# Two-layer mixer encoder: banks copied to SBUF, wide sums of squares, rotations on VectorE, new places for the MLA heads

## The chip, the core and the metric

The kernel runs on one core of a Trainium2 chip. The metric is the device time of one execution in microseconds. A core has TensorE (PE, matrix products, results in PSUM banks of 128 partitions x 512 fp32), ScalarE (ACT), VectorE (DVE), GpSimd (POOL) and SyncE (SP, which here only starts DMA transfers). Each engine works through its own queue in order and waits for others by semaphores.

## What is computed

Two layers over 256 tokens of width 2048, all in fp32. With `rms` a normalisation by the root of the mean square and a gain, each layer is

```python
h = rms_norm(x, norm_mix)
z = einsum('bsd,de->bse', h, w_in)          # split into ten parts
y_a = mlstm_mixer(...)                       # 4 heads, two directions, gates, dv = 128
y_b = mla_mixer(...)                         # 6 heads: q (128 + 64 rotated) from a 384 latent, k and v from a 128 latent
y_c = dilated_mixer(...)                     # 6 heads, softmax over three dilated bands
x = x + einsum('bse,ed->bsd', concatenate([y_a, y_b, y_c]), w_out)
h = rms_norm(x, norm_ff)
u = relu(einsum('bsd,df->bsf', h, w_ff1))
return x + einsum('bsf,fd->bsd', u * u, w_ff2)
```

In `mla_mixer` both latents are normalised, each head's q and k parts are normalised over their own columns, the 64-wide parts are rotated (`x1*cos - x2*sin`, `x2*cos + x1*sin`), and a full softmax attention follows.

## The kernel before

**Products.** Every fp32 operand is split into a high part that TensorE takes at full rate (fp32r) and the rest: high x high, high x low, low x high, three products in place of one. Weights come as tiles of 128 x 1024 fp32 (512 KB) by SP's DMA queue. `Weights.next` keeps three tiles staged (`wst`) and splits three units ahead: ScalarE casts `whi`, VectorE subtracts `wlo`. One such unit feeds 12 products of 512 columns (`token_group`). Tokens are two tiles of 128 (`tt`).

**Stages of a layer.** `mixers` runs nine groups of eight units over `w_in`: group 0 the latents (512 columns), group 1 narrow (336 columns: the 64 rotated k columns, gates, part of the dilated v), groups 2 to 4 the mLSTM q/k, v and output gate, 5 to 7 dilated q/k by pairs of heads, 8 the rest of dilated v. Then `out_proj`, then `ffn` in four chunks. In the first layer x comes transposed (`xt`), and `first_xg` makes the operands and the sums of squares of the first norm on POOL (`sq`, `acc`); `token_factor` turns them into the factor `rt` that evictions apply.

**The order of the work** is fixed while the program is written out. Small work is a set of generator tasks in `Stream`. `issue` keeps a clock for each engine from the prices in `Engine.COST`, `product` one for TensorE; a task's next step is due when its last operation is priced to have ended, plus `MARGIN`, and `pump` inserts the steps that are due between products. `finish`, `until` and `start` do not wait for a due time: they write out the steps of other tasks at once until a condition holds. Rooms are counted (`take`, `give`): `m` for the four PSUM banks of small work, `t2` and `half` for SBUF tiles.

**MLA heads.** `mla_head` starts at places `MLA_AT`, (group, unit), as hooks in `token_group`, through `start`, so it needs its room at that place: two banks, three `t2`, three of seven `half`. It keeps its two banks until the normalised q and k (`nk`) are written. Six squares with accumulated sums on ScalarE give the norms, POOL rotates (`apply_rope`), then transposes (`nkT`, `qrT`), scores (`mla_s`), softmax, transposes of it (`pT`) and the product with v (`oT`). In the profile's line column all ScalarE, VectorE and POOL operations have line 98 (the call in `Engine`), products line 194 (`mm`) and transposes line 200; so the tiles' names tell operations apart.

```python
MLA_AT = ((2, 3), (2, 7), (3, 3), (3, 7), (4, 3), (4, 7))
MLA_ROOM = dict(m=2, t2=3, half=3)
self.until(lambda: all(self.room[k] >= v for k, v in room.items()))   # in Stream.start
```

Of the kernel before, what the change touches and what calls it, by code (L numbers as in the profile page):

```python
# [66 lines left out]
T2, HALF = 22, 7  # L67

MLA_AT = ((2, 3), (2, 7), (3, 3), (3, 7), (4, 3), (4, 7))
MARGIN = 0.4  # L70


class Engine:
# [3 lines left out]
        "activation": (0.16, 0.00083), "copy": (0.07, 0.00083), "tensor_tensor": (0.07, 0.00104),  # L77
        "scalar_tensor_tensor": (0.13, 0.00104), "tensor_scalar": (0.07, 0.00080), "tensor_copy": (0.07, 0.00104),
        "tensor_reduce": (0.07, 0.00104), "tensor_tensor_reduce": (0.07, 0.00104), "reciprocal": (0.07, 0.0066),
        "tensor_tensor_scan": (0.07, 0.00104), "memset": (0.07, 0.0004),  # L80
    }

# [3 lines left out]
    def __getattr__(self, f):  # L86
# [4 lines left out]
        def call(*args, **kw):  # L91
            out = kw["in_"] if f == "tensor_reduce" else kw["out"] if "out" in kw else args[0]
            n = math.prod(out.shape[1:])
            fixed, each = self.COST[f]
            if self.name == "pool":
                fixed, each = 0.15, 2 * each
            self.s.issue(self.name, fixed + each * n)
            return fn(*args, **kw)  # L98
# [18 lines left out]
class Stream:  # L117
# [98 lines left out]
class Weights:  # L216
# [7 lines left out]
    def load(self):  # L224
# [111 lines left out]
def first_xg(c, xg, kt, src, gain):  # L336
# [11 lines left out]
    c.s.cur.last.pop("pool", None)  # L348
# [5 lines left out]

def next_xg(c, xg, g, ss, col):

    nc = c.nc
    for tt in range(NT):
        j = c.tmp.tile([P, 512], F32, tag="junk5", name="junk5", bufs=1)
        nc.scalar.activation(j, c.x[tt][:, g * 512:(g + 1) * 512], AF.Square, accum_out=ss[:, tt, g:g + 1])  # L360
# [72 lines left out]
def token_factor(c, rt):  # L433
# [54 lines left out]
def latents(c, ps, rt, tf):  # L488

    nc = c.nc  # L490
    yield from c.s.take(t2=4)
    while not tf.over:
        yield
# [3 lines left out]
    for tt in range(NT):  # L497
        nc.scalar.activation(z[:, tt, :MLA_QR], ps[tt][:, :MLA_QR], AF.Square, scale=rt[:, tt:tt + 1],
                             accum_out=ss[:, tt:tt + 1])
        nc.scalar.activation(z[:, tt, MLA_QR:], ps[tt][:, MLA_QR:512], AF.Square, scale=rt[:, tt:tt + 1],  # L500
# [9 lines left out]
    for tt in range(NT):  # L510
        nc.scalar.activation(z[:, tt, :MLA_QR], ps[tt][:, :MLA_QR], AF.Copy, scale=f[:, 0, tt:tt + 1])
        nc.scalar.activation(z[:, tt, MLA_QR:], ps[tt][:, MLA_QR:512], AF.Copy, scale=f[:, 1, tt:tt + 1])
# [823 lines left out]
```

## Time and profile before

| | us |
|---|---|
| median of three runs | 2157.35 (2154.82 to 2157.42) |
| the profiled execution | 2155.49 |
| its span, first to last instruction | 2153.3 |
| PE busy | 2119.8 (98%) |
| DVE, ACT, POOL busy | 1322.4, 1082.3, 110.4 |
| mean granted TensorE clock | 0.997 |

The profiled execution lies 1.9 us below the median and 2.2 us above its own span. Busy is the union of an engine's records; a product's record lasts longer than the distance to the next product's start, because products overlap. The stages by the stretches of the trace: the first layer's groups 0 and 1 end near 48 us, its other mixer groups near 291, its output projection near 380, its FFN near 1070; the second layer repeats this, 1360 and 1448 being the ends of its mixers and projection.

### The profile page before, as it was taken

To read this page: it belongs to the slowest core of one execution; us is meant where nothing else is said; L and a number is where in the kernel's file an instruction comes from. 1 tells how busy PE (TensorE), PEld (TensorE's weight loads), DVE (VectorE), ACT (ScalarE), POOL (GpSimd) and SP (SyncE) were. 2 spreads that over 40 slices of the span, in tenths; PEclk is the share of its full clock that TensorE was granted. 3 is DMA by queue.
4 is the path that set the end of the run, shared out by engine and by line. 5 is a ranking of instruction groups with operands and counts; after the bars stand their busy time and mean duration, and the time that the engine had idled before them with its cause. 6 is when DMAs were issued, how large, how long until landed. Compare 5 with 4: busy or idle time off the path is not lost.

```text
span 2153.3 us, 28894 instructions
## 1 busy us (share of the span) xinstructions
PE 2119.8 (98%) x10848; PEld 1804.9 (84%) x10848; DVE 1322.4 (61%) x1963; ACT 1082.3 (50%) x1883; POOL 110.4 (5%) x142
## 2 busy tenths in 40 slices
PE   8999999999999999999999999999999999999999
PEld 6788888888888888888887888888888888888887
DVE  7668755655564565565557687556546655655654
ACT  5666655543453444454456676554434434534442
POOL 6112100000000000000001121000000000000000
PEclk9999999999999999999999999999999999999999
DMA  7544455566656666566554444556565666566565
GB/s 228 189 141 126 154 175 181 187 194 190 193 186 195 194 188 193 190 192 196 178 174 142 143 128 153 174 189 192 186 198 189 190 191 195 187 195 194 187 200 162
DMA packets 109004, 389.89 MB, mean 181 GB/s; under 512 B 12352, under 2 KB 12480, under 8 KB 108608
## 3 DMA queue, kind: packets, MB, share of 16 engines
q1 hardware_dynamic: 107136, 384.97, 56.6%
q10 hardware_dynamic: 1728, 3.07, 0.4%
q8 instruction: 85, 1.39, 0.3%
q14 instruction: 55, 0.45, 0.1%
HBM read 385.90 MB, written 2.10 MB: 180 GB/s over the span
## 4 chain that ended last, share of the span: by engine, by line
PE 89%; ACT 4%; DVE 3%; POOL 2%; issue 1%; DMA 1%; POOLq 0%; ACTq 0%; DVEq 0%; SPq 0%
PE g L194 84%; ACT junk L98 1%; PE mla_z L194 1%; ACT whi L98 1%; DVE wlo L98 1%; POOL acc L98 1%; PE oT L194 1%; POOL sq L98 1%; DMA wst<-w_in 1%; PE xT L200 0%; PE pT L200 0%; PE dil_s L194 0%; PE mla_s L194 0%; POOL rp L98 0%; ACT dil_z L98 0%
## 5 line engine op out<-in xcount | busy, mean ns | idle before, releaser
L98 DVE TENSOR_TENSOR wlo<-wst,whi 128x1024 fp32r<-128x1024 f32 (+2 forms) x732 | 889.5, 1224 | 317.4 <-ACT whi L98 307.7
L98 ACT CAST whi<-wst 128x1024 fp32r<-128x1024 f32 (+2 forms) x732 | 761.2, 1043 | 539.7 <-PE g L194 402.5
L194 PE MATMUL g<-whi,u 128*128 128x512 f32 x2048 | 633.4, 389 | 0.0
L194 PE MATMUL g<-xg,whi 128*128 128x512 f32 x2048 | 489.8, 391 | 0.0
L194 PEld LDWEIGHTS g<-whi,u 128*128 128x128 f32 x2048 | 384.5, 188 | 79.6
L194 PEld LDWEIGHTS g<-xg,whi 128*128 128x128 f32 x2048 | 376.4, 188 | 72.8
L194 PE MATMUL g<-wlo,u 128*128 128x512 f32 x1024 | 398.4, 389 | 0.0
L194 PE MATMUL g<-whi,xg 128*128 128x512 f32 (+1 forms) x1152 | 371.7, 389 | 6.3 <-ACT whi L98 6.3
L194 PEld LDWEIGHTS g<-xg,wlo 128*128 128x128 f32 x2048 | 263.1, 191 | 12.1 <-ACT xg L98 2.0
L194 PE MATMUL g<-xg,wlo 128*128 128x256 f32 x2048 | 267.4, 283 | 1.1 <-ACT xg L98 1.1
L194 PEld LDWEIGHTS g<-whi,xg 128*128 128x128 f32 x1152 | 215.5, 189 | 44.0 <-ACT whi L98 6.3
L194 PEld LDWEIGHTS g<-wlo,u 128*128 128x128 f32 x1024 | 192.3, 188 | 39.8
L194 PE MATMUL g<-wlo,xg 128*128 128x512 f32 (+1 forms) x576 | 222.0, 385 | 3.3 <-DVE wlo L98 3.3
L98 ACT COPY ev<-g 128x256 f32<-128x256 f32 x128 | 48.0, 375 | 340.7 <-PE g L194 340.7
L98 DVE TENSOR_TENSOR ev<-g,ev 128x256 f32<-128x256 f32 x128 | 54.4, 425 | 229.8 <-ACT ev L98 229.7
L194 PE MATMUL g<-whi,y 128*128 128x512 f32 x512 | 162.8, 393 | 0.0
L194 PEld LDWEIGHTS g<-wlo,xg 128*128 128x128 f32 x576 | 109.1, 189 | 23.3 <-DVE wlo L98 6.7
L194 PEld LDWEIGHTS g<-whi,y 128*128 128x128 f32 x512 | 96.1, 188 | 19.7
L194 PE MATMUL g<-wlo,y 128*128 128x512 f32 x256 | 99.7, 389 | 0.0
L98 DVE SCALAR_TENSOR_TENSOR x<-g,r,x 128x512 f32<-128x512 f32 x64 | 45.8, 751 | 83.2 <-PE g L194 83.2
L98 DVE SCALAR_TENSOR_TENSOR ev<-ev 128x256 f32<-128x256 f32 x128 | 54.4, 425 | 4.4
L194 PEld LDWEIGHTS g<-wlo,y 128*128 128x128 f32 x256 | 48.1, 188 | 9.5
(206 smaller groups left out, 1199.1 us busy)
## 6 DMA issues: line engine op xcount, KB each, us to landing
wst<-w_ff SPq DMA_DIRECT2D x512, 512.0 KB, 4.2
wst<-w_in SPq DMA_DIRECT2D x128, 512.0 KB, 3.7
wst<-w_out SPq DMA_DIRECT2D x64, 512.0 KB, 4.2
wst<-w_in SPq DMA_DIRECT2D x16, 336.0 KB, 3.0
wst<-w_mla SPq DMA_DIRECT2D x12, 416.0 KB, 3.1
xt<-xT SPq DMA_DIRECT2D x8, 256.0 KB, 5.1
x<-x SPq DMA_DIRECT2D x2, 1024.0 KB, 7.1
out<-x ACTq DMA_DIRECT2D x8, 256.0 KB, 2.2
```

What stands on the lines that cost most here:

```text
L98: return fn(*args, **kw)
L194: c.nc.tensor.matmul(out, lhsT, rhs, start=start, stop=stop)
```

## The change

- The prices in `COST` are raised, an engine's operations may overlap by 0.08 us, ScalarE's accumulated sums get a price, `MARGIN` is 0.3 in place of 0.4, and a product is priced at n/2400 + 0.0133 us.
- `latents` and `mla_head` copy their PSUM banks to SBUF at once and give them back; MLA gets two SBUF tiles `z` (room `z`), `half` has 9 tiles in place of 7, `t2` 21 in place of 22; an MLA head takes two `t2`. At most two mLSTM heads run at a time (`ml`).
- Sums of squares of MLA and dilated heads: one wide square on ScalarE, then `tensor_reduce` on VectorE.
- `apply_rope` and the gains of the output gate move from POOL to VectorE. The cast of v's high part moves from VectorE to ScalarE.
- `MLA_AT` becomes (3,2), (3,3), (3,7), (4,3), (5,0), (6,1).
- The squares of the first norm move from POOL, beside group 0, to ScalarE and VectorE, after group 0. What needs `rt` in group 1 becomes a task, `narrow`; `finish(tf)` goes.
- The first x load goes to ScalarE's DMA queue, the first weight tile is loaded and split in two halves, ten products of 128 columns stand at the program's start, and the tokens' two loads of 1 MB move from before group 2 to before groups 4 and 5.
- In the very last unit all products of the first token tile stand ahead of those of the second.

```diff
-T2, HALF = 22, 7
-MLA_AT = ((2, 3), (2, 7), (3, 3), (3, 7), (4, 3), (4, 7))
-MARGIN = 0.4
+T2, HALF, MLA_Z, JUNK = 21, 9, 2, 2
+MLA_AT = ((3, 2), (3, 3), (3, 7), (4, 3), (5, 0), (6, 1))
+MARGIN = 0.3
+ML_AT_ONCE = 2
+WARM = 10
...
-        "activation": (0.16, 0.00083), "copy": (0.07, 0.00083), "tensor_tensor": (0.07, 0.00104),
+        "activation": (0.26, 0.00086), "copy": (0.19, 0.00084), "tensor_tensor": (0.155, 0.00105),
...
-    c.s.product(n / 2400.0 * (1 if lhsT.dtype == F32R else 4) + 0.0025)
+    c.s.product(n / 2400.0 + 0.0133 if lhsT.dtype == F32R else n / 1200.0 + 0.0025)
...
+    def pieces(self, i):
+        n = self.srcs[i][1]
+        return [slice(0, n // 2), slice(n // 2, n)] if i == 0 else [slice(0, n)]
...
 def first_xg(c, xg, kt, src, gain):
...
-        sq = c.tmp.tile([P, S], F32, tag="sq", name="sq", bufs=1)
-        nc.gpsimd.tensor_tensor(out=sq, in0=src, in1=src, op=ALU.mult)
-        nc.gpsimd.tensor_tensor(out=c.acc, in0=c.acc, in1=sq, op=ALU.add)
...
+def square(c, src):
+    sq = junk5(c)[:, :src.shape[-1]]
+    c.nc.scalar.activation(sq, src, AF.Square)
+    return sq
...
+def token_factor(c, rt, first):
...
+        xs = [t.rearrange("p i s -> p (i s)") for t in c.xts]
+        for i in range(0, len(xs) + 2, 2):
+            for a in xs[i:i + 2]:
+                nc.scalar.activation(a, a, AF.Square)
+            for a in xs[max(i - 2, 1):i]:
+                nc.vector.tensor_tensor(out=xs[0], in0=xs[0], in1=a, op=ALU.add)
+            yield
...
+def warm_up(c):
+    ones = c.big.tile([P, P], F32, tag="big", name="ones")
+    c.nc.vector.memset(ones, 1.0)
+    ps = new_bank(c, "warm")
+    for _ in range(WARM):
+        c.nc.tensor.matmul(ps[:, :P], ones, ones, start=True, stop=True)
...
 def latents(c, ps, rt, tf):
...
+    for tt in range(NT):
+        nc.scalar.copy(z[:, tt], ps[tt])
     yield from c.s.take(t2=4)
     while not tf.over:
         yield
...
 def apply_rope(c, out, x, cos, sin, n, rot):
...
-    nc.gpsimd.tensor_tensor(out=v1, in0=x, in1=cos, op=ALU.mult)
+    nc.vector.tensor_tensor(out=v1, in0=x, in1=cos, op=ALU.mult)
...
+def narrow(c, ps, rt, tf):
+    while not tf.over:
+        yield
...
+    c.s.spawn(dil_v(c, [p[:, 80:G1_W] for p in ps], rt, slice(0, 256)))
+    c.s.spawn(k_rope(c, z1))
+    c.s.spawn(ml_gates(c, z1))
...
-MLA_ROOM = dict(m=2, t2=3, half=3)
+MLA_ROOM = dict(m=2, t2=2, half=3, z=1)
...
+    for tt in range(NT):
+        nc.scalar.copy(z[:, tt], ps[tt][:, :WZ])
+    c.s.give(m=2)
...
-            nc.scalar.activation(junk(c, b - a), ps[tt][:, a:b], AF.Square, accum_out=ss[:, i, tt:tt + 1])
+    sq = [square(c, z[:, tt, :WQ + MLA_NOPE]) for tt in range(NT)]
...
+            nc.vector.tensor_reduce(out=ss[:, i, tt:tt + 1], in_=sq[tt][:, a:b], op=ALU.add, axis=AX.X)
...
+    nc.scalar.copy(vh, zv)
     apply_rope(c, qr, qr, c.rope[:, 0], c.rope[:, 1], NT, MLA_ROPE)
+    nc.vector.tensor_tensor(out=vl, in0=zv, in1=vh.bitcast(F32), op=ALU.subtract)
...
     for tt in range(NT):
         transpose(c, tq[:MLA_ROPE, tt * P:(tt + 1) * P], qr[:, tt])
     yield
+    c.s.give(z=1)
...
 def dil_prep(c, ps, rt, pair):
...
-        for i in range(4):
-            nc.scalar.activation(junk(c, DIL_DH), z[:, tt, i], AF.Square, accum_out=ss[:, tt, i:i + 1])
+        sq = square(c, z[:, tt].rearrange("p a b -> p (a b)"))
+        yield
+        nc.vector.tensor_reduce(out=ss[:, tt], in_=sq.rearrange("p (a b) -> p a b", a=4), op=ALU.add, axis=AX.X)
...
+            nc.vector.tensor_tensor(out=o, in0=o, in1=c.vec[:, V_ON + h * ML_DV:V_ON + (h + 1) * ML_DV], op=ALU.mult)
...
 def ml_head(c, h):
...
+    yield from c.s.take(t2=2, half=1, ml=1)
     kk, qq, ql = c.mlqk[h]
-    yield from c.s.take(t2=2, half=1)
...
     ps = in_group(c, G1_W)
-    s.finish(tf)
...
-    if after:
-        after()
+    c.kr = None
+    s.spawn(narrow(c, ps, rt, tf))
...
     s.spawn(ml_v(c, ps, rt))
+    if after:
+        after(0)
     ps = in_group(c, 512, hooks(4))
+    if after:
+        after(1)
...
+            if last_layer and ch == NCHUNK - 1 and g == NX - 1:
+                token_group(c, us, ps, 512, range(KT // 2 - 1))
+                last_unit(c, us, ps, 512)
...
+    load_x(nc.scalar)
+    c.w.load()
+    for i in range(c.B_ST - 1):
         load_x()
         c.w.load()
```

## Rows read from the trace of the kernel before

**Rows 1.** Page, part 1: busy us and share of the span of each engine.

```profile
PE 2119.8 (98%) x10848; PEld 1804.9 (84%) x10848; DVE 1322.4 (61%) x1963; ACT 1082.3 (50%) x1883; POOL 110.4 (5%) x142
```

**Rows 2.** Stretches: us, busy of PE, PEld, DVE, ACT, POOL, clock, DMA share, GB/s.

```profile
6.34:12.39 6.05, 5.35 (x12) 3.88 (x13) 6.05 (x6) 4.87 (x9) 5.66 (x6) 1.00 1.01 368
12.39:36.40 24.01, 21.57 (x94) 16.41 (x92) 20.44 (x19) 10.39 (x16) 22.29 (x25) 1.00 0.74 244
36.40:48.00 11.60, 11.60 (x79) 11.58 (x79) 7.58 (x18) 7.58 (x21) 5.52 (x14) 1.00 0.58 166
48.00:98.00 50.00, 47.58 (x259) 39.86 (x258) 33.84 (x80) 34.64 (x91) 3.89 (x7) 1.00 0.60 200
98.00:110.00 12.00, 8.90 (x45) 7.27 (x45) 8.03 (x18) 7.12 (x23) 1.80 (x3) 0.72 0.30 87
110.00:161.00 51.00, 50.35 (x292) 43.31 (x291) 34.67 (x76) 33.02 (x93) 6.88 (x10) 1.00 0.46 148
161.00:291.00 130.00, 125.90 (x669) 106.12 (x668) 101.50 (x229) 85.84 (x237) 21.40 (x20) 1.00 0.45 142
1166.00:1178.00 12.00, 8.71 (x45) 7.33 (x44) 8.07 (x17) 6.77 (x21) 2.16 (x3) 0.72 0.28 91
1178.00:1360.00 182.00, 177.33 (x965) 150.51 (x965) 136.61 (x307) 119.88 (x332) 28.07 (x30) 1.00 0.46 145
```

**Rows 3.** Timeline of the start: start us, us, engine, operation.

```profile
4.09 0.91 ACT L98 ACTIVATE xg<-xt,vec 128x256 fp32r<-128x256 f32 x2 [2.08 <-DMA vec<-vecs]
...
6.34 0.80 PE L194 MATMUL g<-whi,xg 128*128 128x512 f32 x1 [6.34 <-ACT whi L98]
...
7.83 0.79 PE L194 MATMUL g<-wlo,xg 128*128 128x512 f32 x1 [0.70 <-DVE wlo L98]
```

**Rows 4.** Waits of PE: us in total, times, longest us.

```profile
PE pT L200 <- DVE sm_e L98: 5.4, 2, 2.9
PE dqkT L200 <- POOL dil_z L98: 4.4, 4, 1.2
```

**Rows 5.** VectorE's groups, 6.3 to 36.4 us: busy us, mean ns.

```profile
L98 DVE TENSOR_TENSOR wlo<-wst,whi 128x1024 fp32r<-128x1024 f32 x8 | 13.3, 1671 | 0.1
```

**Rows 6.** VectorE's groups, 48 to 380 us.

```profile
L98 DVE TENSOR_TENSOR wlo<-wst,whi 128x1024 fp32r<-128x1024 f32 x92 | 113.3, 1244 | 25.0 <-ACT whi L98 24.6
...
L98 DVE TENSOR_TENSOR y<-oT,y 128x256 fp32r<-128x256 f32 x12 | 5.0, 422 | 6.3 <-ACT y L98 6.3
...
L98 DVE TENSOR_REDUCE sm<-mla_s 128x2 f32<-128x512 f32 x6 | 4.1, 690 | 6.6 <-PE mla_s L194 6.6
...
L98 DVE TENSOR_TENSOR mla_vl<-mla_z,mla_vh 128x128 fp32r<-128x128 f32 x12 | 3.5, 291 | 0.4
```

**Rows 7.** ScalarE's groups, 48 to 380 us.

```profile
L98 ACT CAST whi<-wst 128x1024 fp32r<-128x1024 f32 x93 | 96.7, 1050 | 49.8 <-PE g L194 23.2 <-DMA wst<-w_in 17.7 <-DMA wst<-w_out 5.1
...
L98 ACT CAST p_hi<-pT 128x512 fp32r<-128x512 f32 x12 | 7.0, 591 | 12.8 <-PE pT L200 12.8
...
L98 ACT ACTIVATE junk<-mla_z 128x128 f32<-128x128 f32 x24 | 6.7, 278 | 1.0 <-PE mla_z L194 0.5
...
L98 ACT ACTIVATE junk<-x 128x512 f32<-128x512 f32 x8 | 5.0, 629 | 1.8 <-DVE x L98 1.7
```

**Rows 8.** POOL's groups, whole span.

```profile
L98 POOL TENSOR_TENSOR rp<-dil_z,drope 128x256 f32<-128x256 f32 x12 | 17.9, 1511 | 108.2 <-DVE dil_z L98 102.2 <-DVE ml_den L98 6.0
```

**Rows 9.** Timeline, first layer: a weight cast; the first MLA head.

```profile
63.88 1.05 ACT L98 CAST whi<-wst 128x1024 fp32r<-128x1024 f32 x1 [5.00 <-DMA wst<-w_in]
...
67.26 0.34 PE L194 MATMUL mla_z<-whi,lat_hl 128*128 128x192 f32 x1
...
90.61 0.38 PE L200 MATMUL qrT<-const,qr 128*64 128x128 f32 x2
...
103.67 0.58 PE L194 MATMUL oT<-p_hi,mla_vh 128*128 128x256 f32 x1 [0.25 <-ACT p_hi L98]
```

**Rows 10.** Timeline of the end.

```profile
2148.61 1.43 DVE L98 SCALAR_TENSOR_TENSOR x<-g,r,x 128x512 f32<-128x512 f32 x2 [7.89 <-PE g L194]
```

More of the change, by code (lines that the diff above doesn't have):

```diff
@@ L95, in call @@
             if self.name == "pool":
-                fixed, each = 0.15, 2 * each
-            self.s.issue(self.name, fixed + each * n)
+                fixed, each = 0.3, 4 * each
+            elif self.name == "act" and kw.get("accum_out") is not None:
+                fixed += self.READ
+            self.s.issue(self.name, fixed + each * n, self.OVERLAP)
             return fn(*args, **kw)
@@ L352, in first_xg, with junk5, squares @@
     xg[kt] = hl
+def junk5(c):
+    return c.tmp.tile([P, 512], F32, tag="junk5", name="junk5", bufs=JUNK)
+def square(c, src):
+    sq = junk5(c)[:, :src.shape[-1]]
+    c.nc.scalar.activation(sq, src, AF.Square)
+    return sq
+def squares(c, tt, g, ss):
+    j = junk5(c)
+    c.nc.scalar.activation(j, c.x[tt][:, g * 512:(g + 1) * 512], AF.Square, accum_out=ss[:, tt, g:g + 1])
 def next_xg(c, xg, g, ss, col):
@@ L358, in next_xg @@
     for tt in range(NT):
-        j = c.tmp.tile([P, 512], F32, tag="junk5", name="junk5", bufs=1)
-        nc.scalar.activation(j, c.x[tt][:, g * 512:(g + 1) * 512], AF.Square, accum_out=ss[:, tt, g:g + 1])
+        squares(c, tt, g, ss)
     for half in range(2):
@@ L380, in two_banks, with last_unit @@
     return [c.gps.tile([P, 512], F32, tag="g", name="g") for _ in range(NT)]
+def last_unit(c, acts, ps, w):
+    hi, lo = c.w.next()
+    for tt in range(NT):
+        for j in range(2):
+            kt = KT - 2 + j
+            wh, wl = hi[:, j * w:(j + 1) * w], lo[:, j * w:(j + 1) * w]
+            xh = acts[kt][:, tt * P:(tt + 1) * P]
+            xl = acts[kt][:, S + tt * P:S + (tt + 1) * P]
+            mm(c, ps[tt], xh, wh, False, False)
+            mm(c, ps[tt], xh, wl, False, False)
+            mm(c, ps[tt], xl, wh, False, j == 1)
+            c.s.pump()
 def token_group(c, acts, ps, w, kps=range(KT // 2), hooks=None, prepare=None):
@@ L630, in mla_head @@
         c.s.give(t2=4)
+    z = c.zp.tile([P, 2 * WZ], F32, tag="mla_zs", name="mla_zs").rearrange("p (t w) -> p t w", t=NT)
     ps = []
@@ L637, in mla_head @@
             else:
-                o, cs, first, last = b[:, WQ:WQ + 256], slice(NK * WQ, NK * WQ + 256), True, True
+                o, cs, first, last = b[:, WQ:WZ], slice(NK * WQ, NK * WQ + 256), True, True
             xh = c.lat[kt][:, tt * P:(tt + 1) * P]
@@ L699, in mla_head @@
     p = yield from softmax(c, sc, (MLA_NOPE + MLA_ROPE) ** -0.5, None)
-    yield from pv(c, p, [(vh[:, st], vl[:, st]) for st in range(NT)], 4 + h, 3)
+    yield from pv(c, p, [(vh[:, st], vl[:, st]) for st in range(NT)], 4 + h, 2)
     c.s.give(half=3)
@@ L998, in ml_head @@
     split(c, c.y[h], tp[:, :S])
-    c.s.give(m=1, t2=1, half=1)
+    c.s.give(m=1, t2=1, half=1, ml=1)
 def mixers(c, prepare, after):
@@ L1014, in mixers @@
     ps = in_group(c, 512, prepare=prepare)
-    tf = s.spawn(token_factor(c, rt))
+    tf = s.spawn(token_factor(c, rt, after))
     lat = s.spawn(latents(c, ps, rt, tf))
     ps = in_group(c, G1_W)
-    s.finish(tf)
-    z1 = c.cp.tile([P, NT, MLA_ROPE + 16], F32, tag="z1", name="z1", bufs=1)
-    for tt in range(NT):
-        nc.scalar.activation(z1[:, tt], ps[tt][:, :80], AF.Copy, scale=rt[:, tt:tt + 1])
-    s.spawn(dil_v(c, [p[:, 80:G1_W] for p in ps], rt, slice(0, 256)))
-    kr = s.spawn(k_rope(c, z1))
-    s.spawn(ml_gates(c, z1))
-    if after:
-        after()
+    c.kr = None
+    s.spawn(narrow(c, ps, rt, tf))
     def mla0():
         s.finish(lat)
-        s.finish(kr)
+        s.until(lambda: c.kr)
         mla(0)()
@@ L1110, in ff1_end @@
     yield
-    t = c.tmp.tile([P, S], F32, tag="ev1", name="ev1", bufs=2)
+    t = junk5(c)[:, :S]
     nc.scalar.copy(t, ps[:, S:])
@@ L1157, in encoder @@
     c.half = pool("half", HALF)
+    c.zp = pool("zp", MLA_Z)
     c.tmp = pool("tmp", 2)
@@ L1171, in encoder @@
     c.xss = None
-    xts = []
+    c.xts = xts = []
+    c.mean = c.cp.tile([P, 16], F32, tag="mean", name="mean")[:, :2]
+    nc.vector.memset(c.mean, 1.0 / D)
     c.const = c.cp.tile([P, C_ALL], F32, tag="const", name="const")
@@ L1201, in encoder @@
     cr = c.cp.tile([P, C_R], F32R, tag="const_r", name="const_rr")
-    for i in range(c.B_ST):
+    load_x(nc.scalar)
+    c.w.load()
+    for i in range(c.B_ST - 1):
         load_x()
```

116 lines of the change are left out of this document (58 added, 58 removed).

## Prediction, before the changed kernel ran

> **What bounds the kernel now.** I read the page first. TensorE is recorded busy for 2119.8 of 2153.3 us [rows 1], so about 33.5 us of its time are open, and neither ScalarE (50%) nor VectorE (61%) is the bound over the whole span. The change alters no product that the kernel needs, so it can only give back time in which TensorE waits or runs slowly. That is why the second view is the one by stretches: stretch length less PE busy is the idle time, and the clock column shows a slow clock. The stretches of the first layer [rows 2] are: 6.34 us until the first product [rows 3], 0.70 us idle at 6.34 to 12.39, 2.44 us at 12.39 to 36.4, nothing at 36.4 to 48, 2.42 us at 48 to 98, 3.10 us at 98 to 110 together with a mean clock of 0.72, 0.65 us at 110 to 161, and 4.10 us at 161 to 291. Everything outside the mixers is full. The second layer repeats the last three: 3.29 us at 1166 to 1178 (clock 0.72 again) and 4.67 us from there to 1360 [rows 2].
>
> A slow clock is lost time that counts as busy. A stretch of 12 us at 0.72 loses 0.28 x 12 = 3.4 us, once in each layer. At 6.34 to 12.39 the column has no record yet, but 12 products keep PE busy for 5.35 us, 0.45 us each, against 21.57 / 94 = 0.23 us right after: the 1.2 GHz level, some 2.7 us lost. Last, a product's record (0.39 us long, the next one starting 0.23 us after it) covers another 0.16 us of each wait. So the pool is 33.5 + 2 x 3.4 + 2.7, and with some thirty waits 5 us more: about 48 us.
>
> The third view says who ends the waits [rows 4]: softmax values on their way to the transposes (5.4 us), and the rotated dilated heads from POOL (4.4 us in 4 waits, 1.1 us each).
>
> **The change, part by part.** All sums are against the profiled execution: 2155.49 us, its span 2153.3 and 2.2 around it; it lies 1.9 us below the median of 2157.35.
>
> *A, start: -1.2 us (0 to -2.1).* The first product waits for whi: x and the gains land at 4.09, ScalarE makes two tiles of xg, then a whi, 1.05 us [rows 3, 7]. With the first weight tile in two halves its first cast is about 0.6 us long (p_hi, 512 columns, 0.591 [rows 7]), 0.45 less. Against that, the first x now stands behind the gains on ScalarE's queue and may land later, so -0.5. The second product waits for wlo until 7.83, 1.49 us after the first [rows 3]; half a tile, without POOL beside it, is about 0.7: -0.7.
>
> *B, warm-up: -1.2 us (0 to -2.7).* Ten small products at the start can only help the clock. They are short beside the 6 us until the first product, so a pause lies between. Nothing in the trace of before shows activity, a pause and activity again at the start, so the bounds are nothing and the whole 2.7; I take a little under half. The rows show what the clock does after a wait: it fell in the stretch whose waits reach 2.9 us [rows 2, 4] and not at 48 to 98 or 161 to 291, whose named waits are 1.2 us at most [rows 4]. The Trainium skill (TensorE: Matmul & The Clock Gate, "What's actually happening") says that the slow state is the default and that activity releases it; by that rule a warm-up that is followed by a pause is worth nothing for certain, B would be 0 and the sum -20.7.
>
> *C, first group: -3.0 us (-1.5 to -3.5).* While POOL squares x (22.29 of 24.01 us busy), VectorE is at 20.44 of 24.01 [rows 2] and a wlo takes 1.671 us [rows 5], later 1.244 [rows 6]. The idle 2.44 us and the covered part of some seven waits, 1.1 us, are waits for wlo. With POOL silent, a unit costs VectorE 1.24 + 2 x 0.45, some 2.2 us (0.45 is an estimate: a 256-column operation, 0.422 [rows 6], with a gain) against 2.75 us of TensorE (12 x 0.23). One short wait stays. The Trainium skill (SBUF — State Buffer, "Who interferes with whom") states that a VectorE operation with two SBUF inputs is locked out by a GpSimd operation that reads SBUF; by that, all of it comes back, C is -3.5 and the sum -22.4. The row shows 1.671 against 1.244 but not who blocked whom.
>
> *D, second group: +1.0 us (0 to +3).* The squares come back on ScalarE and VectorE after the first group: 8 squares at 0.629 [rows 7] and 8 adds at about 0.69 (a 512-column operation [rows 6]), 5.0 and 5.4 us, beside 7.58 of 11.6 us that either has there now [rows 2]; two bank copies at 0.59 come on top for ScalarE. That is about 14 us of ScalarE in some 15 us of TensorE. The weights are split three units ahead, which hides most of it. If a cast comes late, PE waits; what hangs on the norm comes some 6 us later, which the later MLA start covers.
>
> *E, 48 to 98: -1.7 us (-3 to +2).* ScalarE waits 5.00 us for a weight tile behind the 2 MB of tokens on SP's queue [rows 9]; VectorE stands behind it with that tile's wlo, and what it has queued after that, the gate values, makes most of PE's 2.42 us. One megabyte at a time, ahead of the weights that are loaded when groups 4 and 5 begin, delays a tile half as long on the same queue; the tokens themselves are read only by the output projection, some 150 us later. The forced finish of the norm factor, which drew casts and latents together, goes too. With 0.5 us covered, 2.9; 1.2 stay for the two new loads.
>
> *F, the forced MLA start: -9.5 us (-13 to 0).* At 98 to 110 a head may start only when a head before it has ended: three tiles of seven "half" buffers each, eight units apart. Idle 3.1 + clock 3.4 = 6.5 us, in the second layer 6.7: 13.2. A head lasts from 67.26 to 103.67, 36 us [rows 9]. Afterwards there are nine halves, and the spans are: third head, 5 units + 2 head products after the first, some 21 us, needs the first one's z buffer, which comes free at qrT, now 23 us after the start [rows 9]; fourth head, 9 units and 3 head products, some 36 us, needs the first one's halves. The head itself: POOL's two rotations and sum become three VectorE operations at 0.29 [rows 6], some 1.3 us less; two copies (about 0.55), two squares (about 0.5) and six short sums (about 0.25; estimates from the 512-column and 128-column operations [rows 6, 7]) take the place of six squares (0.278 at most [rows 7], with a read-out each), some 1 us more; but the two banks come free at once. So the third start just misses by some 2 us, too short for the clock to fall: 1.8 us stay in each layer, 13.2 - 3.6 = 9.6, say 9.5.
>
> *G, other mixer waits: -2.0 us (-5 to +6).* Of 4.75 and 4.67 us idle behind 110 and 1178, 2.2 are POOL's (H). The rest, 2.5 a layer, are ML heads and softmax where the planner's prices were short. It had 0.92 us for a cast of 1024 that takes 1.050, now 1.05; 1.14 for a wlo at 1.244, now 1.23 [rows 6, 7]; 0.216 for a product that takes 0.23, now 0.227. Work is then due when it is ready; against it stands a fuller VectorE. One microsecond a layer.
>
> *H, dilated rotations: -4.2 us (-5 to 0).* A POOL step takes 1.511 [rows 8], VectorE's same size 0.422 [rows 6]: the chain shortens by some 3 us against waits of 1.1. 2.2 + 2 x 0.16 = 2.5 a layer, 0.4 stay.
>
> *Nothing:* FFN and output projection (full; their scratch tile changes its name) and the last unit: VectorE's two last operations run from 2148.61 for 1.43 us without a pause [rows 10], and the second begins when the last product ends, so earlier words of the first token tile save about 0.1 (0 to -0.7).
>
> Sum: -1.2 - 1.2 - 3.0 + 1.0 - 1.7 - 9.5 - 2.0 - 4.2 - 0.1 = **-21.9 us**, 2133.6 against the profiled execution, 2135.4 against the median; I take 2134.
>
> **The rivals.**
> *Nearly all waits go:* each term at its better end, B and F whole, about -35: 2120 us. For it: the prices meet the rows. Against: 16 heads still meet the same two engines.
> *VectorE becomes the bound at 161 to 291.* It has 101.5 of 130 us now [rows 2]. To it come rotations (9 x 0.42 + 6 x 0.29 = 5.5), dilated sums (6 x 0.69 = 4.1), MLA sums (3), gate gains (8 x 0.29 = 2.3) and about one head's work moved in (6): some 119 of 133 with what goes. At 89% its queue is long, G and H are lost and 3 us a layer come on top: -21.9 + 6.2 + 6 = -9.7, 2146 us.
> *Forced starts at every later head (slower).* If the second to fourth of the later starts each pay what 98 to 110 pays, 6.5 us, that is 6 x 6.5 = 39 against 13 now: +26, and the other terms give 12.4: +13, 2169 us. It decides from four such stretches on ((13 + 12.4) / 6.5). For it: t2 shrinks from 22 to 21, and only two z buffers. Against: at 110 to 161, where three more heads start, only 0.65 us are idle.
> *It doesn't do what it says:* a wait of like size elsewhere, 2152 to 2159.
>
> **How the numbers follow.** Forecast (2125 to 2144) 0.57; all waits gone 0.17; VectorE 0.13; forced starts 0.08; no change 0.05. A measurement tells 0.2% (4.3 us) from nothing. Faster: 0.57 + 0.17 + 0.11, 0.85; same 0.06; slower 0.09. The range 2118 to 2152 leaves out the forced starts and the ends of two others.
>
> **What would show it.** A: first product before 6.0. B: 12 products from there under 4 us. C: wlo near 1.24 and no wait for it before 36. D: waits for whi or wlo in the 15 us after. F: no clock under 1 in either mixer, heads under 36 us. H: no wait before dqkT over 0.3. Wrong would be: a new stretch with a clock under 1, VectorE over 90% busy for 100 us, or any change in the FFN.

## Result and the profile after

| | before | changed |
|---|---|---|
| median, us | 2156.72 | 2123.51 |
| lowest to highest | 2154.82 to 2157.42 | 2121.99 to 2124.34 |
| profiled execution, us | 2155.49 | 2121.99 |
| its span, us | 2153.3 | 2120.2 |
| mean granted clock | 0.997 | 1.000 |

The changed kernel is faster by 1.5%: ratio 0.9847, 95% interval 0.983 to 0.9864, 33.2 us by the medians. That is inside the range, but 10.5 us below the forecast and only 3.5 us above the rival in which nearly all waits go. The two profiled executions lie 1.2 and 1.5 us below these medians.

The page's engine line of the changed kernel, against [rows 1]: the open time of TensorE went from 33.5 to 10.4 us, the operations of VectorE grew by 12 us, POOL is almost out of use.

```profile
PE 2109.8 (100%) x10868; PEld 1804.6 (85%) x10868; DVE 1334.6 (63%) x2086; ACT 1076.7 (51%) x1728; POOL 14.3 (1%) x35
```

The stretches of the changed kernel, columns as in [rows 2]. The mixers are cut here at 161 and 291 (first layer) and 1230 and 1360 (second):

```profile
6.34:12.39 6.05, 5.12 (x20) 3.77 (x21) 5.70 (x10) 5.94 (x12) 0.00 (x0) 1.00 0.99 372
12.39:36.40 24.01, 24.01 (x120) 20.67 (x120) 15.50 (x23) 15.93 (x26) 7.24 (x16) 1.00 0.79 270
48.00:161.00 113.00, 111.64 (x627) 95.56 (x626) 90.37 (x233) 83.14 (x195) 0.00 (x0) 1.00 0.54 174
161.00:291.00 130.00, 130.00 (x699) 111.28 (x698) 105.95 (x246) 81.56 (x186) 0.00 (x0) 1.00 0.50 156
1118.00:1230.00 112.00, 111.52 (x627) 96.06 (x626) 88.63 (x210) 78.74 (x181) 0.00 (x0) 1.00 0.48 151
1230.00:1360.00 130.00, 130.00 (x689) 110.96 (x689) 100.98 (x226) 80.01 (x174) 0.00 (x0) 1.00 0.51 158
```

At 48 to 161 idle time is 113.00 - 111.64 = 1.36 us with the clock at 1.00; before it was 6.2 us there (48 to 98, 98 to 110 and 110 to 161 in [rows 2]), with a stretch at 0.72. At 161 to 291 nothing is idle, against 4.10 us; that stretch is not quite the same work, since the output projection's first product starts at 258.0 in the changed kernel and at 280.7 before. The second layer is the same: 0.48 and 0 us. VectorE is at 105.95 of 130 us at 161 to 291, against 101.50.

TensorE's waits of the changed kernel, columns as in [rows 4]: softmax on the way to `pT` and the rotated heads on the way to `dqkT` are gone, and a wait for a bank before `mla_z` is 0.2 us.

```profile
PE g L200 <- DVE wlo L104: 1.8, 3, 0.9
PE g L200 <- ACT whi L104: 1.4, 1, 1.4
PE g L200 <- ACT xg L104: 1.1, 2, 0.6
PE warm L510 <- DVE mean L104: 1.0, 1, 1.0
PE qrT L206 <- ACT ml_wt L104: 0.7, 2, 0.4
PE mla_z L200 <- DVE ml_ql L104: 0.2, 1, 0.2
```

Stage lengths, from the first starts of the products of each stage in the two timelines (us). By these starts the kernel before enters its projections at 280.7 and 1348.8, its FFNs at 374.5 and 1442.6 and its second layer at 1083.9, so the stage ends given with its profile are rough by up to 14 us. Some of the dilated heads' work moved behind the mixers, so the output projection grew by 2.4 us a layer.

| stage | before | changed | difference | forecast |
|---|---|---|---|---|
| until the first product | 6.3 | 7.0 | +0.7 | A: -0.5 |
| group 0, first layer | 28.0 | 22.9 | -5.1 | rest of A, B, C: -4.9 |
| groups 1 to 8 and projection, first layer | 340.1 | 324.3 | -15.9 | D to H in both layers: -16.4 |
| FFN, first layer | 709.4 | 709.3 | -0.1 | 0 |
| group 0, second layer | 22.7 | 22.7 | 0 | 0 |
| groups 1 to 8 and projection, second layer | 336.0 | 323.6 | -12.4 | see above |
| FFN and end | 710.7 | 710.4 | -0.2 | -0.1 |

So the start came out as a sum (-4.4 against -5.4), and groups 1 to 8 with the projections gave 28.3 us against 16.4. Idle time and slow clock in the stretches above make 23.2 of the 28.3 (25.0 before, 1.8 left), and one wait of 0.97 us in group 1 is gone too; the other 4 us are not split further. The experiments are about where those come from.

### The profile page after: what moved, and what is told of

Same layout as the page of the kernel before. It is cut to its first block, busy times and chain, and to the rows that moved or that the text cites. A ratio compares the mean times of both kernels' runs of the same rounds, so it can differ in the third digit from the quotient of the medians.

```text
span 2120.2 us, 28690 instructions
## 1 busy us (share of the span) xinstructions
PE 2109.8 (100%) x10868; PEld 1804.6 (85%) x10868; DVE 1334.6 (63%) x2086; ACT 1076.7 (51%) x1728; POOL 14.3 (1%) x35
## 4 chain that ended last, share of the span: by engine, by line
PE 96%; DMA 2%; DVE 1%; ACT 1%; issue 0%; SPq 0%; ACTq 0%; DVEq 0%
PE g L200 90%; PE mla_z L200 2%; DMA wst<-w_in 2%; PE oT L200 1%; PE mla_s L200 1%; DVE wlo L104 1%; PE ml_h L200 1%; PE pT L206 0%; PE xT L206 0%; PE dil_s L200 0%; ACT whi L104 0%; PE nkT L206 0%; PE dqkT L206 0%; PE ml_w L200 0%; PE qrT L206 0%
## 5 line engine op out<-in xcount | busy, mean ns | idle before, releaser
L104 DVE TENSOR_TENSOR wlo<-wst,whi 128x1024 fp32r<-128x1024 f32 (+3 forms) x733 | 881.2, 1211 | 304.5 <-ACT whi L104 295.0
L104 ACT CAST whi<-wst 128x1024 fp32r<-128x1024 f32 (+3 forms) x733 | 761.7, 1041 | 517.5 <-PE g L200 370.1
L104 ACT COPY junk<-g 128x256 f32<-128x256 f32 x128 | 47.9, 374 | 342.3 <-PE g L200 342.3
L104 DVE TENSOR_TENSOR junk<-g,junk 128x256 f32<-128x256 f32 x128 | 54.3, 425 | 231.6 <-ACT junk L104 231.4
L200 PEld LDWEIGHTS g<-whi,y 128*128 128x128 f32 x512 | 96.2, 188 | 19.5
L104 DVE SCALAR_TENSOR_TENSOR junk<-junk 128x256 f32<-128x256 f32 x128 | 54.4, 425 | 4.4
## 6 DMA issues: line engine op xcount, KB each, us to landing
wst<-w_in SPq DMA_DIRECT2D x16, 336.0 KB, 3.1
```

What stands on the lines that cost most here:

```text
L200: c.nc.tensor.matmul(out, lhsT, rhs, start=start, stop=stop)
```

## Experiments

Each was timed against the kernel before on the same chip; "against the changed kernel" is the difference of medians to 2123.51. The medians of the kernel before are 2155.78 to 2156.72 there, so a difference of 1 us says nothing. All stage lengths below are read from the timelines as in the table.

### Parts done alone on the kernel before

**Prices alone.** The whole of `COST`, `MARGIN`, the overlap, the read-out and the product's price as changed.

```diff
-        "activation": (0.16, 0.00083), "copy": (0.07, 0.00083), "tensor_tensor": (0.07, 0.00104),
+        "activation": (0.26, 0.00086), "copy": (0.19, 0.00084), "tensor_tensor": (0.155, 0.00105),
...
-MARGIN = 0.4
+MARGIN = 0.3
```

> The kernel before with the new prices, margin, overlap and product price alone; nothing else changed. Theory P (the waits in the mixers come from prices that were too low, so that transposes were written out before their operands were ready): the waits before pT and dqkT shrink, both clock dips go, 12 to 20 us faster than before, some 2141. Theory R (the large wait at 98 to 110 comes from the room that a starting MLA head needs, whatever the prices): that stretch and its twin at 1166 keep over 2 us of idle and the 1.2 GHz level, only the smaller waits shrink, 3 to 7 us faster, some 2152.

Measured: 2190.58 us, ratio 1.0157 (1.0142 to 1.0172): 34 us *slower*. Neither theory had that. TensorE's waits:

```profile
PE pT L204 <- DVE sm_e L102: 11.3, 7, 4.2
PE g L198 <- DVE wlo L102: 9.9, 9, 3.0
...
PE oT L198 <- ACT p_hi L102: 4.1, 6, 0.7
```

and the stretch:

```profile
48.00:161.00 113.00, 98.61 (x523) 83.90 (x523) 68.21 (x153) 67.64 (x185) 8.48 (x16) 0.92 0.46 146
```

The wait of softmax grew from 5.4 us in 2 [rows 4] to 11.3 us in 7, `oT` waits six times, and a `wlo` comes 3.0 us late. The stretch at 48 to 161 has 14.4 us idle and a clock of 0.92. Only the wait before `dqkT` shrank as P said, from 4.4 to 0.7 us. Prices that meet the rows are no gain by themselves: theory P falls for the kernel before, and R too, since the waits did not shrink but multiply.

**Places alone.**

```diff
-MLA_AT = ((2, 3), (2, 7), (3, 3), (3, 7), (4, 3), (4, 7))
+MLA_AT = ((3, 2), (3, 3), (3, 7), (4, 3), (5, 0), (6, 1))
```

> The kernel before with the new MLA places alone ((3,2), (3,3), (3,7), (4,3), (5,0), (6,1)); prices, banks and rooms as before. Theory R: the heads still need three of seven halves, so the third start at (3,7), some 21 us after the first, is forced harder than before (27 us apart then): the clock dip stays or gets longer, 0 to 8 us slower than before. Theory S (the spacing of the later heads is what counts): the dips go, 8 to 13 us faster. Theory P: within 3 us of before.

Measured: 2176.07 us, ratio 1.0091 (1.0076 to 1.0106), 20 us slower. TensorE's waits, two lines of the view, the place of the second, and a stretch:

```profile
PE oT L194 <- DVE p_lo L98: 6.0, 3, 2.9
PE mla_z L194 <- DVE ml_ql L98: 5.8, 2, 2.9
```

```profile
96.16 0.33 PE L194 MATMUL mla_z<-whi,lat_hl 128*128 128x192 f32 x1 [2.88 <-DVE ml_ql L98]
```

```profile
108.00:126.00 18.00, 14.71 (x78) 12.91 (x78) 9.56 (x23) 9.99 (x30) 2.86 (x5) 0.72 0.17 51
```

Theory S falls. R's sign and its mechanism are there: before the third head, which starts at 123.4, 3.3 us of 18.00 are idle and the clock is at 1.2 GHz from 114.9 to 125.1. But the loss is more than twice R's 8 us, and a second wait, which no theory named, is not one for halves: the head at (3,3) starts its first token tile at 91.76, 5.5 us behind the head at (3,2), and the products of its second token tile wait 2.88 us, in each layer, for a VectorE operation of the mLSTM keys (`ml_ql`). That operation empties one of the four PSUM banks of small work; by the code the head needs two of them, and the head before still holds its own.

**Prices, places and nine halves together** (the three edits above, `HALF` 9, `T2` 21; MLA head and latents of before).

```diff
-T2, HALF = 22, 7
+T2, HALF = 21, 9
```

> The kernel before with new prices, new places and nine half tiles (t2 21) together; MLA head, latents, rotations on POOL, first norm and start as before. Each of the first two alone made it slower. Theory N: together they give most of what the mixers gained, 15 to 22 us faster than before (2134 to 2141), no stretch at 1.2 GHz. Theory K: without the banks given back at once they do not, between 5 us faster and 20 us slower than before.

Measured: 2175.23 us, ratio 1.0092 (1.0075 to 1.0109), 19.5 us slower, at the edge of what theory K had. The same bank wait stands there:

```profile
PE g L198 <- DVE wlo L102: 14.5, 10, 3.1
...
PE mla_z L198 <- DVE ml_ql L102: 5.8, 2, 2.9
```

So more halves, right prices and the new places do not suffice while the head stays as it was, and theory N falls. That its banks are the reason is not shown by this run: the waits for `wlo` are the longer ones here, 14.5 us.

**Rotations on VectorE alone.**

```diff
-    nc.gpsimd.tensor_tensor(out=v1, in0=x, in1=cos, op=ALU.mult)
+    nc.vector.tensor_tensor(out=v1, in0=x, in1=cos, op=ALU.mult)
...
```

> The kernel before with the rotations (three operations of apply_rope) on VectorE in place of POOL, nothing else. By the prediction's term H: the four waits before dqkT (4.4 us, 1.1 each) go to 0.3 or less and 4 to 5 us are gained, some 2152.5. Rival: VectorE's fuller queue makes wlo or softmax late instead, gain under 1 us.

Measured: 2159.41 us, ratio 1.0012 (1.0003 to 1.0021): 3 us slower. The waits before `dqkT` are gone from the view, as H said, but softmax took their place, 10.4 us in 4 waits where it was 5.4 in 2:

```profile
PE pT L200 <- DVE sm_e L98: 10.4, 4, 3.0
```

### Parts undone in the changed kernel

In the profiled executions of the first five runs below, group 0 of the first layer takes 24.0 to 25.2 us against 22.9 in the changed kernel's. So 1 to 2 us of a difference can lie in the start, which varies as the runs on the warm-up below show, and not in the part undone.

**Seven halves.**

```diff
-T2, HALF, MLA_Z, JUNK = 21, 9, 2, 2
+T2, HALF, MLA_Z, JUNK = 21, 7, 2, 2
```

> The changed kernel with seven half tiles in place of nine; all else as changed. Theory R: the third MLA head cannot start at (3,7) before the first has ended, some 21 us after that one's start against a head's 30 or more: a forced stretch comes back in each layer, with the clock at 1.2 GHz, 10 to 20 us slower than the changed kernel (2134 to 2143). Theory P: within 2 us of the changed kernel (2123).

Measured: 2141.85 us, 18.3 us against the changed kernel, R's figure. The third head starts at 111.5 in place of 100.8, and a forced run of `mla_s` and `pT` stands before it; the clock falls to 1.2 GHz once in each layer (0.98 of 113 us and 0.98 of 112 us):

```profile
PE pT L206 <- DVE sm_e L104: 4.1, 4, 1.6
...
PE mla_s L200 <- ACT qrT_sb L104: 2.1, 2, 1.1
```

and its stretches:

```profile
48.00:161.00 113.00, 108.90 (x597) 93.14 (x597) 84.08 (x216) 79.81 (x182) 0.00 (x0) 0.98 0.52 166
...
1118.00:1230.00 112.00, 107.90 (x588) 92.20 (x587) 82.70 (x203) 72.90 (x154) 0.00 (x0) 0.98 0.47 148
```

**The MLA head of before** in the changed kernel: banks kept until q and k are normalised, accumulated sums, three `t2` of 22, no `z`, v's high part cast on VectorE.

```diff
-    for tt in range(NT):
-        nc.scalar.copy(z[:, tt], ps[tt][:, :WZ])
-    c.s.give(m=2)
...
+    for i in range(2):
+        a, b = cols[i]
+        for tt in range(NT):
+            nc.scalar.activation(nk[:, i, tt], ps[tt][:, a:b], AF.Copy, scale=r[:, 2 * i + tt:2 * i + tt + 1])
+    c.s.give(m=2)
```

> The changed kernel with the MLA head of before: it keeps its two banks until q and k are normalised, sums its squares with ScalarE's accumulator, and takes three t2 tiles of 22 and no z; places, nine halves, prices, rotations on VectorE and the rest as changed. Theory K (giving the banks back at once is what lets two heads start one unit apart): the start at (3,3) and those after it are forced, a stretch at 1.2 GHz in each layer, 10 to 25 us slower than the changed kernel (2134 to 2149). Theory N (halves, places and prices suffice): within 4 us of 2123.

Measured: 2162.99 us, 39.5 us against the changed kernel and, at 1.0034 (1.0021 to 1.0047) of the kernel before, slower than that. Theory N falls; the sign and the bank waits are K's, the size is beyond its 10 to 25 us. The run undoes several things at once, so the 39.5 us are not those of the banks alone. The clock has a mean of 0.94 at 48 to 161, and waits for `mla_z` are back, for three different holders of banks:

```profile
PE mla_z L200 <- DVE ml_ql L104: 4.3, 3, 2.8
...
PE mla_z L200 <- ACT sm_e L104: 2.0, 2, 1.0
PE mla_z L200 <- DVE ml_em L104: 1.8, 1, 1.8
```

**Narrow sums on the copied banks.** The copies stay; the six sums of an MLA head go back to ScalarE's accumulator.

```diff
-    sq = [square(c, z[:, tt, :WQ + MLA_NOPE]) for tt in range(NT)]
+    for tt in range(NT):
+        for i, (a, b) in enumerate(((0, MLA_NOPE), (WQ, WQ + MLA_NOPE), (MLA_NOPE, WQ))):
+            nc.scalar.activation(junk(c, b - a), z[:, tt, a:b], AF.Square, accum_out=ss[:, i, tt:tt + 1])
```

> The changed kernel with the sums of squares of the MLA heads as six squares with ScalarE's accumulator on the copied banks, in place of two wide squares and six sums on VectorE; the copies of the banks stay. Theory K (it is the banks given back at once, not the wide sums, that the undone MLA head lost): within 3 us of the changed kernel. Rival (the wide sums carry it, through the length of the head): 8 us slower or more.

Measured: 2138.08 us, 14.6 us against the changed kernel. So the sums carry a good part too: "within 3 us" was wrong, and the rival's 8 us or more came. No bank wait of over 0.5 us comes back. The second head reaches `qrT` 10.7 us later (115.2 against 104.5) although it starts 2 us later only, and short waits stand all over the mixers:

```profile
PE g L200 <- DVE wlo L104: 4.9, 7, 1.0
PE ml_st L200 <- ACT ml_wt L104: 2.2, 2, 1.1
...
PE nkT L206 <- DVE dil_k L104: 1.6, 2, 0.8
...
PE mla_z L200 <- DVE ml_wt L104: 0.9, 2, 0.5
```

ScalarE's groups of that run, 48 to 380 us (busy us, mean ns), show what six sums cost: squares and read-outs of their own, (7.5 + 3.1 + 6.8) / 6 = 2.9 us of ScalarE a head. In the changed kernel the same view has 5.0 us of ScalarE for the wide squares and 8.2 us of VectorE for their sums, 2.2 us a head. The head's own chain differs by 0.7 us only; that 14.6 us hang on it means that other work is written out elsewhere, and how that comes about is not shown.

```profile
L104 ACT ACTIVATE junk<-mla_zs 128x128 f32<-128x128 f32 x24 | 7.5, 312 | 0.6
...
L104 ACT ACTIVATION_READ_ACCUMULATOR junk<-mla_zs 128x1 f32 x36 | 6.8, 188 | 0.0
...
L104 ACT ACTIVATE junk<-mla_zs 128x64 f32<-128x64 f32 x12 | 3.1, 257 | 0.4
```

**Old prices of the operations** in the changed kernel; margin and product price stay as changed.

```diff
-        "activation": (0.26, 0.00086), "copy": (0.19, 0.00084), "tensor_tensor": (0.155, 0.00105),
+        "activation": (0.16, 0.00083), "copy": (0.07, 0.00083), "tensor_tensor": (0.07, 0.00104),
...
-    OVERLAP, READ = 0.08, 0.2
+    OVERLAP, READ = 0.0, 0.0
...
-                fixed, each = 0.3, 4 * each
+                fixed, each = 0.15, 2 * each
```

> The changed kernel with the old prices of the operations of ScalarE, VectorE and POOL, no overlap and no price for a read-out; margin 0.3 and the product's price as changed. Theory P (right prices are needed once the rooms are there): transposes are written out before their operands are ready again, waits before pT and oT return, 5 to 15 us slower than the changed kernel. Theory R (rooms decide): within 3 us.

Measured: 2130.00 us, 6.5 us against the changed kernel. In the second layer groups 1 to 8 take 227.8 us against 227.4 and the projection 1.3 us less: no loss at all. In the first layer groups 1 to 8 are 8.9 us longer, most of it at one place, where latents, `narrow` and casts meet behind the norm factor:

```profile
60.03 1.21 DVE L104 TENSOR_TENSOR wlo<-wst,whi 128x1024 fp32r<-128x1024 f32 x1
...
61.30 0.80 PE L200 MATMUL g<-wlo,xg 128*128 128x512 f32 x1 [3.81 <-DVE wlo L104]
```

In the 3.81 us before that product the clock falls, for 6.8 us. The time is P's (5 to 15 us slower), but of the waits that P named only one of 0.9 us before `pT` is there, and none before `oT`; R's 3 us are passed, mainly by that one place.

**Rotations back on POOL** in the changed kernel, all three operations.

```diff
-    nc.vector.tensor_tensor(out=v1, in0=x, in1=cos, op=ALU.mult)
+    nc.gpsimd.tensor_tensor(out=v1, in0=x, in1=cos, op=ALU.mult)
...
```

> The changed kernel with the three operations of apply_rope back on POOL (priced as the changed kernel prices POOL). By term H: 4 to 5 us slower than the changed kernel, with waits before dqkT of 1 us each. Rival, after the run of the rotations alone: a chain that is longer by 3 us only shifts the dates of the transposes, and where heads have room nothing waits for them: within 2 us.

Measured: 2130.06 us, 6.5 us against the changed kernel, a little above what H asked, and the rival's 2 us are passed. But no wait before `dqkT` came; in the trace groups 1 to 8 are 6.8 us longer over both layers, and the waits that are new stand at `oT` of an MLA head and at `ml_st`, which are not operations of the dilated heads:

```profile
PE oT L200 <- DVE p_lo L104: 2.4, 2, 1.2
PE ml_st L200 <- ACT ml_wt L104: 2.2, 2, 1.1
```

**Norm on POOL** (with seven halves, since the sum needs the room; read against that kernel's 2141.85).

```diff
+    if kt == 0:
+        c.acc = c.small.tile([P, S], F32, tag="acc", name="acc", bufs=1)
+        nc.gpsimd.tensor_tensor(out=c.acc, in0=src, in1=src, op=ALU.mult)
+    else:
...
+        nc.gpsimd.tensor_tensor(out=sq, in0=src, in1=src, op=ALU.mult)
+        nc.gpsimd.tensor_tensor(out=c.acc, in0=c.acc, in1=sq, op=ALU.add)
...
-        xs = [t.rearrange("p i s -> p (i s)") for t in c.xts]
...
```

> The changed kernel with seven half tiles (as e8_half7, so that the squares' tile has room) and the sums of squares of the first norm on POOL beside group 0, as in the kernel before. Read against e8_half7 (2141.9). By terms C and D: wlo takes 1.6 to 1.7 us again up to 36 us, waits for it return, 1.5 to 3 us slower than e8_half7. If POOL's work was not what made VectorE slow, wlo stays near 1.24 and the time is equal or, since group 1 has less to do, up to 1 us shorter.

Measured: 2147.31 us, 5.5 us slower than seven halves alone, more than the 1.5 to 3 expected. VectorE's `wlo` up to 36.4 us, first with the norm on POOL, then with seven halves alone, and the stretch at 6.34 to 12.39 with the norm on POOL:

```profile
L104 DVE TENSOR_TENSOR wlo<-wst,whi 128x1024 fp32r<-128x1024 f32 x7 | 11.7, 1684 | 0.0
```

```profile
L104 DVE TENSOR_TENSOR wlo<-wst,whi 128x1024 fp32r<-128x1024 f32 x7 | 8.7, 1238 | 4.9 <-ACT whi L104 4.8
```

```profile
6.34:12.39 6.05, 3.60 (x9) 2.67 (x10) 5.95 (x7) 6.05 (x13) 5.58 (x8) 0.72 0.82 279
```

1.684 against 1.238 us for the same operation. TensorE is idle for 2.45 of the 6.05 us and its mean clock is 0.72; group 0 takes 29.6 us in place of 25.0.

**Without the warm-up.**

```diff
-WARM = 10
+WARM = 0
```

> The changed kernel without the ten small products at the start. By term B at its upper bound: the clock rises some 5 to 6 us after the first product, as in the kernel before, and the time is 2 to 3 us longer than the changed kernel's. At its lower bound (the pause undoes the warm-up): no difference.

Measured: 2124.56 us, ratio to before 0.9856 (0.9841 to 0.9871) where the changed kernel has 0.9847: 1.0 us, which this measurement cannot tell from nothing. The profiles show why it is small. Eight profiled variants have the warm-up, the changed kernel among them. In three of them (changed kernel, old prices, x on SP's queue) the granted clock rises to 2.4 GHz at 5.7 to 6.4 us, behind the ten products, and stays. In four (old head, narrow sums, rotations on POOL, norm on POOL) it rises earlier, at 4.3 to 5.5 us while the ten products run, falls at 7.7 to 8.9, when weight products have begun, and rises again at 11.1 to 12.3. With seven halves it rises at 13.5 only. After 7.4 us products follow each other every 0.23 us at the higher level and every 0.43 at the lower. Where the warm-up did not hold, group 0 takes 24.0 to 25.2 us (29.6 with the norm on POOL), about the 24.1 without any warm-up or more. The stretch from 7.4 to 11.4 us in the changed kernel, and in the one with the old MLA head:

```profile
7.40:11.40 4.00, 3.78 (x16) 2.77 (x16) 3.67 (x8) 3.89 (x8) 0.00 (x0) 1.00 1.01 388
```

```profile
7.40:11.40 4.00, 3.77 (x10) 2.88 (x10) 3.22 (x6) 3.47 (x7) 0.00 (x0) 0.60 1.03 394
```

**First x on SP's queue.**

```diff
-    load_x(nc.scalar)
+    load_x()
```

> The changed kernel with the first x load on SP's queue, ahead of the first weight tile, as in the kernel before; the rest as changed. The changed kernel's first product starts at 7.04, because that x, third in line for the DMA engines, lands at 5.5. If the order of the loads is the cause, x lands at about 4, the first product starts at 5.9 to 6.3 and the time is 0.7 to 1.2 us shorter than the changed kernel's. If the DMA engines' sum is the limit, the first weight half lands later instead, and nothing is gained.

Measured: 2124.11 us, 0.6 us against the changed kernel. x lands as early as said and the first product starts at 5.56, but group 0 then takes 26.7 us in place of 22.9: the later tiles are late by what the first one gained and more.

```profile
5.56 0.64 PE L200 MATMUL g<-whi,xg 128*128 128x512 f32 x1
...
10.04 0.49 PE L200 MATMUL g<-whi,xg 128*128 128x512 f32 x1 [0.96 <-ACT whi L104]
...
11.29 0.50 PE L200 MATMUL g<-wlo,xg 128*128 128x512 f32 x1 [0.76 <-DVE wlo L104]
```

## Why the prediction was right, and where not

*A* had the wrong sign for the first product. It starts at 7.04, not before 6.0: x as third transfer is there at 5.58 only. The step that failed is "may land later, so -0.5": the lateness was named and given no price, and it came to more than the 0.45 us that the half cast saves. The 16 DMA engines are full there (a share of 0.99 at 6.34 to 12.39 above), and moving one load moves the lateness on, as the run with x on SP's queue shows. The second product's part held: 0.73 us behind the first, against 1.49 [rows 3].

The timeline of the start, changed kernel, as [rows 3]:

```profile
1.05 4.64 PE L510 MATMUL warm<-ones 128*128 128x128 f32 x20 [1.05 <-DVE mean L104]
...
5.58 0.91 ACT L104 ACTIVATE xg<-xt,vec 128x256 fp32r<-128x256 f32 x2 [3.56 <-DMA xt<-xT]
...
7.04 0.50 PE L200 MATMUL g<-whi,xg 128*128 128x512 f32 x1 [1.36 <-ACT whi L104]
...
7.77 0.50 PE L200 MATMUL g<-wlo,xg 128*128 128x512 f32 x1 [0.22 <-DVE wlo L104]
```

*B* is right as a bound, and the profiled execution met its upper end by luck: 20 products in 5.12 us at 6.34 to 12.39, 12 before [rows 2], and 12 products from the first one in 3.4 us. As a term it is 1.0 us, which cannot be told from nothing. The three profiles that stay at 2.4 GHz are those with the shortest pauses between the warm-up and the first weight product: 0 (x on SP's queue), 1.10 (old prices) and 1.36 us (changed kernel); the others had 1.45 to 2.11 us. They are also those in which the clock rose latest of the seven that rose early, and a rise during the ten products ends these sooner, which makes the pause longer. So the pause is not shown as the cause. The Trainium skill (TensorE: Matmul & The Clock Gate, "What's actually happening") states that the slow state is the default and that activity releases it; the rise during or right behind the ten products agrees in seven of eight profiles, and the one with seven halves (13.5 us) does not show it. That a pause makes a warm-up worth nothing, which the prediction drew from the rule, it does not say. The prediction's "1.2 us at most" for the waits at 48 to 98 left out one of 1.81 us before `ml_aT` at 66.91, at which the clock did not fall either.

*C* and *D*: no wait is left at 12.39 to 36.4, so C came at its upper end, 3.5; D, +1.0, did not come, ScalarE and VectorE hold the second group with 0.31 us idle up to 65 (24.01 of 24.01, 11.60 of 11.60, 16.69 of 17.00). Together -3.5 against -2.0, and 5.5 by the run with the norm on POOL, where the waits also cost clock. One reading of C was wrong: of its 2.44 us "waits for wlo", 0.97 is a wait of the norm's own product (`stat`, 35.92) for POOL's last sum. The rule of the Trainium skill (SBUF — State Buffer, "Who interferes with whom"), that a VectorE operation with two SBUF inputs contends with a GpSimd operation that reads SBUF, fits: with POOL squaring beside it, 22.28 of 24.01 us at 12.39 to 36.4, the same VectorE operation takes 1.684 in place of 1.238 us.

*E* was not tried alone. At 48 to 98 the idle time went from 2.42 to 0.88 us, near the forecast, but with other work in the stretch. TensorE's three waits for `wlo` in the changed kernel lie at 7.77, 65.3 and 1102.7 us, none at a token load (issued at 105.10 and 132.80).

*F* was right that the stretches at 1.2 GHz go, and nine halves were rightly named: without them they come back. Two steps of it failed. "The two banks come free at once" stood there without a price: the old head, which takes back the copies, the wide sums and the rooms together, costs 39.5 us, the narrow sums alone 14.6; the copies by themselves were not timed, and as the parts are not additive the difference is not their price. The other step is the third start, which was to miss the z buffer by 2 us and keep 1.8 us a layer. The first head reaches `qrT` 20.0 us after its start (80.58 to 100.61), where I had kept the 23 of before; so z comes free just in time and the third head waits for nothing. A whole head did not get shorter: first products to `oT` took 37.2 us (80.58 to 117.81) against 36.4 [rows 9].

The timeline of the changed kernel, stations of the first head and the start of the third (100.75), as [rows 9]:

```profile
80.58 0.33 PE L200 MATMUL mla_z<-whi,lat_hl 128*128 128x192 f32 x1 [0.22 <-DVE ml_ql L104]
...
100.61 0.38 PE L206 MATMUL qrT<-const,mla_zs 128*64 128x128 f32 x2
100.75 0.34 PE L200 MATMUL mla_z<-whi,lat_hl 128*128 128x192 f32 x1
...
117.81 0.28 PE L200 MATMUL oT<-p_hi,mla_vh 128*128 128x256 f32 x1
```

*G* named the wrong cause. Prices that meet the rows made the kernel before 34 us slower, and the old ones cost the changed kernel 6.5 us in one place. At 161 to 291, where nothing is idle in the changed kernel, 5.3 us are idle with the old head, 1.9 with seven halves and 1.1 with the old prices: the head and its room took more of these waits away than the prices.

*H* was near in size only inside the changed kernel (6.5 us) and not in place; alone it cost 3 us where -4.2 was promised. Its mark (no wait before `dqkT` over 0.3 us) was met in every run on the changed kernel, with the rotations on POOL too, so it marks nothing.

*The other marks:* no clock under 1 in a mixer and an untouched FFN were met, VectorE stayed below 90%; heads under 36 us were not.

*The rival of a full VectorE* was mis-sized: 119 us at 161 to 291 was said, 105.95 came. At 48 to 161 VectorE has 90.37 us against 76.5 (the sum of its three stretches in [rows 2]), and the later stretch now holds 33 us of output projection against 10; how much each of the two took off is not worked out. *Forced starts* did not come in the changed kernel, but its mechanism stands in three of the runs: with seven halves, the old head or the new places alone, later starts are forced or wait for banks, and with the places alone the time is even above the 2169 us of that rival.

So the sum was 11.6 us short (33.5 against 21.9, profiled executions), and all of it is in D to H. That the total still lay in the range is in part luck: G's reason was wrong, and what F rests on had no price. In the mixers of before, 18.2 us were idle and 6.8 lost to the clock, 25.0 together [rows 2]; 1.8 are left, and I had left some 8. I had priced the parts one by one against the schedule of before, and they are not additive. Undone one at a time in the changed kernel, halves, head, prices and rotations cost 18.3, 39.5, 6.5 and 6.5 us; done alone before, prices, places and rotations cost 34, 20 and 3 us. Why right prices alone do so much harm is argued, not shown: a later date leaves more of a head undone when the next start forces it out. Neither tried alone nor undone were the copies of the latents, the wide sums of the dilated heads, the moved gains, the limit of two mLSTM heads, `narrow`, the token loads and the last unit; what they hold of the 11.6 us is open.

## What to carry to other kernels

When small work is written out between large products, look first at what a start has to own (banks, buffers): a forced start writes steps out together, and here the prices, the places and the rotations, each tried without that room, only moved the waits to other names. Price a set of scheduling edits as a set; the rotations are worth 6.5 us in the finished arrangement and cost 3 us on their own. Read a stall's place as a symptom: the line that ends it says which operand came last, not which room was missing.

## What the runs showed of the hardware

A short warm-up of TensorE before the first weights gave the higher clock for good in three of eight profiles only (rise at 5.7 to 6.4 us); in four the clock rose at 4.3 to 5.5 and fell again at 7.7 to 8.9, in one it rose at 13.5. It is worth 1.0 us here, which cannot be told from nothing. In one wait of 3.81 us the clock fell to 1.2 GHz, for 6.8 us (old prices); with seven halves it fell at 109.0, for 3.4 us, behind waits of 1.1, 0.6 and 1.6 us (103.07, 104.21 and 108.10). In the first microseconds the DMA engines are full whichever load goes first: a share of 0.99 and 372 GB/s at 6.34 to 12.39 in the changed kernel, 1.00 and 376 with x on SP's queue, 1.01 and 368 before. A square on ScalarE that also sums has a second record, the read-out of the sum: 188 ns beside 312 ns for the 128x128 square.
